# A decoder step on one core: the first weights and the first memory tile taken in smaller pieces, the second memory tile issued by SyncE, a shorter lead-in

## The chip, the core and the metric

The kernel runs on one core of one Trainium2 chip. The metric is the device time of one execution in microseconds. A core has a matrix engine (TensorE; PE in the profile, its weight loads PEld), VectorE (DVE), ScalarE (ACT), GpSimd (POOL) and SyncE (SP), which here only issues DMAs. Sixteen DMA engines move data between HBM and the on-chip memory.

## What is computed

The reference is one layer of a decoder with three parallel branches (a convolution, stick-breaking attention, softmax attention into 256 memory tokens), gates, an output projection and a feed-forward part. Cut to the part at the start of the kernel:

```python
def memory_kv(mem, g_mem, w_mem_kv, g_k_mem):
    b, m, _ = mem.shape
    kv = (rms_norm(mem, g_mem) @ w_mem_kv).reshape(b, m, 2, MEM_HEADS, HEAD_DIM)
    return rms_norm(kv[:, :, 0], g_k_mem), kv[:, :, 1]
...
        mk, mv = memory_kv(mem_prompt, g_mem[l], w_mem_kv[l], g_k_mem[l])
        yp, cp, kp, vp = trunk_layer(yp, zero_hist, no_past, no_past, mk, mv, p)
```

The memory has 256 tokens of 2048 features, and w_mem_kv is 2048 x 1024 (512 columns of keys, 512 of values). Everything is float32.

## The kernel before, in words

All weights lie in HBM as 504 slabs of 128 partitions x 1024 float32 (512 KB each), in the order of their use. A slab is loaded by SyncE (`load_slab`, line 290) into one of four raw buffers. ScalarE then casts it to a rounded high part (line 312), and VectorE subtracts the two to get the low part (line 323). The activations are split in the same way, and a product is the sum of three matmuls: high x high, low x high, high x low. Each of the three runs in the rounded format fp32r.

The first stage is `mem_products` (line 573): the memory's keys and values. The contraction runs over 16 tiles of 128 features. Two feature tiles share a pair of slabs: slab 2 k2 holds their value columns and slab 2 k2 + 1 their key columns, the first 512 columns of a slab for the even feature tile and the last 512 for the odd one. A turn is one feature tile with one slab half: six matmuls with 512 moving columns (line 594), for two blocks of 128 memory tokens. The turns begin (tile 0, values), (tile 0, keys), (tile 1, values), (tile 1, keys). So turns one and two use the first halves of slabs 0 and 1, turns three and four their second halves.

The memory tile of a feature tile is 128 x 256. `prep_mem` (line 345) scales it by the gain into a high part, for tile 0 on VectorE (line 350), for all others on ScalarE (line 354). `prep_low` (line 371) makes the low part on VectorE. The slabs of this stage are taken in two halves of 256 KB. Memory tiles 0 and 1 are loaded by two DMAs that ScalarE issues ahead of everything (lines 247 and 248); tile 0 carries 48 columns of gains. The other memory tiles are issued by SyncE (line 406), among the slab halves: memory tile, value slab half, key slab half, and so on.

TensorE begins with `warm_up` (line 1500): ten matmuls on a constant, nine of 512 columns and one of 256, whose result is not used.

The order on every engine is written out when the program is built, by a small planner (`Order`, line 76). Each job asks for an engine with an estimated cost and with flags that it waits for, and the planner runs them in simulated time. What comes out is a fixed instruction stream for each engine. The costs and flags fix the order only; on the chip, semaphores hold back an instruction until its data are there.

Of the kernel before, what the change touches and what calls it, by code (L numbers as in the profile page):

```python
# [15 lines left out]
P = 128  # L16
D_MODEL = 2048
KT = D_MODEL // P
# [8 lines left out]
ML = 256  # L27
MT = ML // P
# [8 lines left out]
SLAB = 8 * P  # L37
N_SLABS = 504


C_GMIX, C_GMEM, C_GMLP, C_BGATE = 0, 16, 32, 48
# [113 lines left out]
def dve(n, *flags, **take):  # L155
    return Ask("DVE", 0.18 + n / 920.0, flags, **take)


def act(n, *flags, **take):
    return Ask("ACT", 0.22 + n / 1200.0, flags, **take)  # L160
# [6 lines left out]
def pe(us, *flags, **take):  # L167
    return Ask("PE", us, flags, **take)


def sp(*flags, **take):
    return Ask("SP", 0.45, flags, **take)
# [7 lines left out]
MM_MEM = 0.226  # L180
# [3 lines left out]
def tile_decoder_step(ctx: ExitStack, tc: tile.TileContext, xT, memT, wall, cvec, kmat, ptab,  # L184
                      kpool, vpool, mkc, mvc, hist,
                      yT, oK, oV, oCp, oCs, oMK, oMV):
    nc = tc.nc
# [15 lines left out]
    order = Order(bufs)  # L203
    give, add, done = order.give, order.add, order.set
# [38 lines left out]
    cm = tl("k4", [P, 1024])  # L243
# [1 line left out]
    order.pools["s"].pop()  # L245
    order.pools["k4"].pop()
    nc.scalar.dma_start(cm[:, :C_BGATE + ML], memT[:, :C_BGATE + ML])
    nc.scalar.dma_start(first[:, 1], memT[:, C_BGATE + ML:C_BGATE + 2 * ML])
    nc.gpsimd.tensor_copy(cv[:, :C_BGATE], cm[:, :C_BGATE])
    km = cpool.tile([P, NKM], F32, name="km")  # L250
    pt = cpool.tile([1, 2 * NB], I32, name="pt")
# [22 lines left out]


    class Slab:
        def __init__(self, parts):
            self.parts = parts
            self.landed = [Flag() for _ in range(parts)]
            self.split = [Flag() for _ in range(parts)]  # L280

    slabs = [Slab(2 if s < 2 * KT // 2 else 1) for s in range(N_SLABS)]
    at_slab = [0, 0.0]

    def load_slab(s, part):
        sl = slabs[s]
        if part == 0:
            sl.raw = tl("wr", [P, SLAB])
        n = SLAB // sl.parts
        nc.sync.dma_start(sl.raw[:, part * n:(part + 1) * n], wall[s, :, part * n:(part + 1) * n])  # L290
        sl.landed[part].at = order.landed(n * P * 4 / 1e3)

    def shifted(p, s):
        n = 0 if s < 2 * KT // 2 else SHIFT
# [5 lines left out]
    cast_at, sub_at = [0], [0]  # L300

    def cast_weights():
        todo = [(0, 0), (1, 0), (0, 1), (1, 1)] + [(s, i) for s in range(2, N_SLABS) for i in range(slabs[s].parts)]
        for s, i in todo:
            sl = slabs[s]
            n = SLAB // sl.parts
            cast_at[0] = s
            yield act(n, sl.landed[i], **({} if i else {"w": 1}))
            if i == 0:
                sl.h = shifted("wh", s)  # L310
            c = slice(i * n, (i + 1) * n)
            nc.scalar.copy(sl.h[:, c], sl.raw[:, c])  # L312
            sl.split[i].cast = order.now.ready
            add(sub_part(s, i), lambda s=s: 0 if due(s) - order.free["DVE"] < 5.0 else 4.5)

    def sub_part(s, i):
        sl = slabs[s]
        n = SLAB // sl.parts
        yield dve(n, late=Order.HOP + 0.1)
        if i == 0:  # L320
            sl.l = shifted("wl", s)
        c = slice(i * n, (i + 1) * n)
        nc.vector.tensor_sub(sl.l[:, c], sl.raw[:, c], sl.h[:, c].bitcast(F32))  # L323
        done(sl.split[i])
        if i == sl.parts - 1:
            give("wr")

    def start_slab(s):
        at_slab[:] = [s, order.now.ready]
# [10 lines left out]
    hm, hx = [None] * KT, [None] * KT  # L340
    hm_in, hx_in = [Flag() for _ in range(KT)], [Flag() for _ in range(KT)]
    mem_sum, x_sum = [], []
    sums_m, sums_x, km_in = Flag(), Flag(), Flag()

    def prep_mem(k2, raw, here):
        for i in range(2):
            if k2 + i == 0:
                yield dve(ML, here[i], a=2)
                a = hm[0] = Acts(ML)
                nc.vector.tensor_scalar_mul(a.h, raw[:, i], cm[:, C_GMEM:C_GMEM + 1])  # L350
            else:
                yield act(ML, here[i], a=2)
                a = hm[2 * k2 + i] = Acts(ML)
                nc.scalar.mul(a.h, raw[:, i], col(C_GMEM + 2 * k2 + i))
            add(prep_low(a, raw[:, i], C_GMEM + 2 * k2 + i, ML, hm_in[2 * k2 + i]), 0.5 + 0.01 * k2)
        yield act(2 * ML, hm_in[2 * k2 + 1])
        if k2 == 0:
            mem_sum.append(tl("s", [P, 512]))
            nc.scalar.activation(mem_sum[0], raw.rearrange("p k t -> p (k t)"), AF.Square)
            give("k4")  # L360
        else:
            nc.scalar.activation(raw, raw, AF.Square)
            yield dve(2 * ML)
            nc.vector.tensor_add(mem_sum[0], mem_sum[0], raw.rearrange("p k t -> p (k t)"))
            give("s")
            if k2 == KT // 2 - 1:
                done(sums_m)
# [24 lines left out]
    def loads():  # L392

        xs = [(0, 3), (3, 6), (6, 9), (9, 12), (12, 15), (15, 16)]
        for k2 in range(KT // 2):
            raw = first
            if k2:
                yield sp(s=1)
                raw = tl("s", [P, 512]).rearrange("p (k t) -> p k t", k=2)
            here = [Flag(), Flag()]  # L400
            for i in range(2):
                for what in ("vmk" if k2 + i == 0 else "mvk"):
                    if what == "m":
                        if k2:
                            yield sp()
                            nc.sync.dma_start(raw[:, i], memT[:, C_BGATE + (2 * k2 + i) * ML:C_BGATE + (2 * k2 + i + 1) * ML])
                        here[i].at = order.landed(131)
                        if i == 0:
                            add(prep_mem(k2, raw, here), 0.5 + 0.01 * k2)
                    else:  # L410
                        yield sp(**({} if i else {"wr": 1}))
                        load_slab(2 * k2 + "vk".index(what), i)
            if k2 >= 1 and xs:
                k0, k1 = xs.pop(0)
                yield sp(k4=1)
                x = tl("k4", [P, 1024])[:, :(k1 - k0) * T].rearrange("p (k t) -> p k t", k=k1 - k0)
                nc.sync.dma_start(x, xT[:, k0:k1, :])
                there = Flag()
                there.at = order.landed(147 * (k1 - k0))
                for k in range(k0, k1):  # L420
                    add(prep_x(k, x[:, k - k0], there, k == k1 - 1), 1.5 + 0.01 * k)
            if k2 == 1:
                yield sp()
                nc.sync.dma_start(cv[:, C_BGATE:], cvec[:, C_BGATE:])
            if k2 == 2:
                yield sp()
                nc.sync.dma_start(km, kmat)
                km_in.at = order.landed(213)
                yield sp()
                nc.sync.dma_start(pt, ptab)  # L430
                pt_in.at = order.landed(1) + 20.0
        for s in range(KT, N_SLABS):
            yield sp(wr=1)
            load_slab(s, 0)
# [138 lines left out]
    def mem_products():  # L573
        yield pe(0.0, pm=4)
        pv, pk = [bank("pm") for _ in range(MT)], [bank("pm") for _ in range(MT)]
        add(mem_values(pv), 1.0)
        add(mem_keys(pk), 0.9)
        turns = [(0, 0), (0, 1), (1, 0), (1, 1)]
        turns += [(2 * k2 + i, x) for k2 in range(1, KT // 2) for x in range(2) for i in range(2)]
        slab_no[0] += KT  # L580
        for k, x in turns:
            ps, flag = ((pv, vflag), (pk, kflag))[x]
            s = 2 * (k // 2) + x
            sl = slabs[s]
            w = slice(k % 2 * MW, (k % 2 + 1) * MW)
            yield pe(6 * MM_MEM, sl.split[k % 2], hm_in[k])
            if k % 2 == 0:
                start_slab(s)
            a = hm[k]
            todo = [(a.h, sl.h, 0), (a.h, sl.h, 1), (a.l, sl.h, 0), (a.l, sl.h, 1), (a.h, sl.l, 0), (a.h, sl.l, 1)]  # L590
            if k == 0:
                todo = todo[:2] + todo[4:] + todo[2:4]
            for j, (y, z, m) in enumerate(todo):
                nc.tensor.matmul(ps[m], y[:, m * P:(m + 1) * P], z[:, w],  # L594
                                 start=(k == 0 and j < 2), stop=(k == KT - 1 and j in (4, 5)))
            if k % 2:
                give("w")
            if k == KT - 1:
                done(flag)
            if k % 2 and x:  # L600
                give("a", 4)
# [897 lines left out]

    def warm_up():  # L1500

        yield pe(4.2, pa=1)
        junk = bank("pa")
        one = nc.const_aps.tensor(1.0, [P, 512], mybir.dt.bfloat16)
        for n in [512] * 9 + [256]:
            nc.tensor.matmul(junk[:, :n], one[:, :P], one[:, :n], start=True, stop=True)
        give("pa")

# [201 lines left out]
```

## Time and profile before

| What | Value |
|---|---|
| Median of 3 runs | 1618.26 us (1618.14 to 1618.41) |
| Span of the profiled execution, first to last instruction | 1616.7 us |
| TensorE busy in the span | 1612.4 us, 12657 matmuls |
| VectorE busy | 1003.4 us |
| ScalarE busy | 771.5 us |
| GpSimd busy | 138.4 us |
| Moved by DMA | 310.25 MB, mean 192 GB/s |

The times in the profile count from the first instruction of the execution. In a row of a timeline stand the start, the duration, the engine, the line of the kernel, the operation, the tile written and the tiles read, and in brackets how long the engine was idle before it and what ended that. A q behind the name of an engine means that its sequencer issues a DMA. The shares of busy time are means over the whole span; for a change of the first microseconds it is the rows of the first microseconds that matter, and what follows on the chain of work that ended last.

### The profile page before, as it was taken

Reading aid. Unit: us, or ns where it says so; the run is one execution under the profiler, and the core shown is the slowest. Engines: PE = TensorE matmul, PEld = TensorE weight load, DVE = VectorE, ACT = ScalarE, POOL = GpSimd, SP = SyncE. Lnnn points to the kernel's source line nnn. Section 1 sums busy time; section 2 is a strip of 40 time slices with the busy share of each in tenths; the row PEclk is TensorE's granted clock in tenths of the full one; section 3 lists DMA queues with packets and bytes.
Section 4 is the critical chain, followed back from the end, with each engine's and each line's share of the span. In section 5 each row is a group of like instructions: output and inputs, shape, how many; then the busy total and the mean of one; then the engine's idle time right before and its main releaser. Section 6 shows DMA issues by size and latency. Waiting matters only on the chain.

```text
span 1616.7 us, 30794 instructions
## 1 busy us (share of the span) xinstructions
PE 1612.4 (100%) x12657; PEld 1595.2 (99%) x12657; DVE 1003.4 (62%) x1469; ACT 771.5 (48%) x1106; POOL 138.4 (9%) x107
## 2 busy tenths in 40 slices
PE   9999999999999999999999999999999999999999
PEld 7999999999999999999999999999999999999999
DVE  7999888887777655655555544555445554455443
ACT  8856887775433634444443333333333333333332
POOL 0020000000000000002222100121002210022100
PEclk9999999999999999999999999999999999999999
DMA  9898678978755555566655555555555555555563
GB/s 325 224 211 279 174 224 245 342 213 296 217 171 162 166 176 171 152 192 193 192 172 169 170 170 170 170 170 170 169 169 168 171 168 167 172 165 168 180 192 100
DMA packets 127200, 310.25 MB, mean 192 GB/s; under 512 B 40018, under 2 KB 49618, under 8 KB 127058
## 3 DMA queue, kind: packets, MB, share of 16 engines
q1 hardware_dynamic: 126770, 307.98, 63.0%
q8 instruction: 99, 1.62, 0.4%
q14 instruction: 43, 0.35, 0.1%
q10 hardware_dynamic: 288, 0.29, 0.1%
HBM read 296.99 MB, written 6.32 MB: 188 GB/s over the span
## 4 chain that ended last, share of the span: by engine, by line
PE 99%; DMA 0%; ACT 0%; DVE 0%; issue 0%
PE pm L541 93%; PE pm L594 3%; PE pa L541 1%; PE pl L1102 1%; PE pl L1286 0%; PE pa L929 0%; DMA wr<-in_wall 0%; PE pa L930 0%; PE pa L931 0%; PE pl L1116 0%; PE pa L1226 0%; PE pa L1262 0%; PE pa L889 0%; ACT wh L312 0%; DVE a L1456 0%; PE pl L1324 0%
## 5 line engine op out<-in xcount | busy, mean ns | idle before, releaser
L312 ACT CAST wh<-wr 128x1024 fp32r<-128x1024 f32 (+1 forms) x520 | 530.6, 1023 | 628.3 <-PE pm L541 568.8
L541 PE MATMUL pm<-a,wh 128*128 128x288 f32 x5184 | 735.2, 292 | 0.0
L323 DVE TENSOR_TENSOR wl<-wr,wh 128x1024 fp32r<-128x1024 f32 (+1 forms) x520 | 618.3, 1192 | 185.5 <-ACT wh L312 181.6
L541 PEld LDWEIGHTS pm<-a,wh 128*128 128x128 f32 x5184 | 695.4, 188 | 0.4 <-issue 0.4
L541 PE MATMUL pm<-a,wl 128*128 128x288 f32 x2592 | 395.3, 292 | 0.0
L541 PEld LDWEIGHTS pm<-a,wl 128*128 128x128 f32 x2592 | 357.5, 188 | 0.2 <-issue 0.2
L541 PE MATMUL pm<-k,wh 128*128 128x288 f32 x2400 | 337.8, 292 | 0.0
L541 PEld LDWEIGHTS pm<-k,wh 128*128 128x128 f32 x2400 | 321.0, 188 | 0.0
L541 PE MATMUL pm<-k,wl 128*128 128x288 f32 x1200 | 182.0, 292 | 0.0
L541 PEld LDWEIGHTS pm<-k,wl 128*128 128x128 f32 x1200 | 165.1, 188 | 0.0
L1442 POOL TENSOR_TENSOR t<-t 128x288 f32<-128x288 f32 x64 | 95.6, 1495 | 600.4 <-DVE t L1439 600.4
L1456 DVE TENSOR_TENSOR a<-a,pm 128x288 f32<-128x288 f32 x64 | 29.1, 455 | 122.7 <-PE pm L541 122.7
L1439 DVE SCALAR_TENSOR_TENSOR t<-pm,rx 128x288 f32<-128x288 f32 x64 | 29.2, 458 | 90.7 <-PE pm L541 90.7
L1445 ACT CAST k<-t 128x288 fp32r<-128x288 f32 x60 | 25.8, 432 | 123.4 <-POOL t L1442 123.4
L1358 DVE TENSOR_TENSOR t<-pm,rx 128x288 f32<-128x288 f32 x48 | 22.0, 458 | 68.3 <-PE pm L541 68.3
L1447 DVE TENSOR_TENSOR k<-t,k 128x288 fp32r<-128x288 f32 x60 | 27.8, 466 | 58.2 <-ACT k L1445 58.2
L773 DVE SCALAR_TENSOR_TENSOR a<-a,cv,a 128x256 f32<-128x256 f32 x120 | 59.6, 496 | 1.3
L1428 POOL TENSOR_TENSOR t<-t,t 128x288 f32<-128x288 f32 x15 | 21.6, 1440 | 416.1 <-ACT t L1425 416.1
L594 PE MATMUL pm<-wh,a 128*128 128x512 f32 x128 | 34.6, 393 | 0.3 <-ACT wh L312 0.3
L541 PE MATMUL pm<-s,wh 128*128 128x288 f32 x160 | 33.7, 292 | 0.0
L594 PEld LDWEIGHTS pm<-wh,a 128*128 128x128 f32 x128 | 24.2, 190 | 5.9 <-ACT wh L312 1.0
L541 PEld LDWEIGHTS pm<-s,wh 128*128 128x128 f32 x160 | 25.3, 188 | 0.0
(203 smaller groups left out, 756.7 us busy)
## 6 DMA issues: line engine op xcount, KB each, us to landing
wr<-in_wall SPq DMA_DIRECT2D x488, 512.0 KB, 3.7
wr<-in_wall SPq DMA_DIRECT2D x32, 256.0 KB, 5.1
k<-in_kpool SPq DMA_DIRECT2D x32, 256.0 KB, 5.9
k<-in_vpool SPq DMA_DIRECT2D x32, 256.0 KB, 5.9
k<-in_mkc SPq DMA_DIRECT2D x8, 512.0 KB, 7.4
k<-in_mvc SPq DMA_DIRECT2D x8, 512.0 KB, 7.7
t<-in_xT SPq DMA_DIRECT2D x16, 144.0 KB, 3.7
out_yT<-a SPq DMA_DIRECT2D x16, 144.0 KB, 1.9
```

Of the source, the lines that this page charges most:

```text
L312: nc.scalar.copy(sl.h[:, c], sl.raw[:, c])
L323: nc.vector.tensor_sub(sl.l[:, c], sl.raw[:, c], sl.h[:, c].bitcast(F32))
L541: nc.tensor.matmul(ps, w, a, start=(first and i == 0), stop=(last and i == len(todo) - 1))
L594: nc.tensor.matmul(ps[m], y[:, m * P:(m + 1) * P], z[:, w], start=(k == 0 and j < 2), stop=(k == KT - 1 and j in (4, 5)))
L773: nc.vector.scalar_tensor_tensor(c[:, :NP], up[:, k:k + NP], w, c[:, :NP], op0=ALU.mult, op1=ALU.add)
L1358: nc.vector.tensor_mul(g, ps, rx)
L1428: nc.gpsimd.tensor_add(sq_sum[0], sq_sum[0], res[0])
L1439: nc.vector.scalar_tensor_tensor(r, ps, 0.0, r2, op0=ALU.max, op1=ALU.mult)
L1442: nc.gpsimd.tensor_mul(r, r, r)
L1445: nc.scalar.copy(a.h, r)
L1447: nc.vector.tensor_sub(a.l, r, a.h.bitcast(F32))
L1456: nc.vector.tensor_add(x1[j], x1[j], ps)
```

## The change

1. The DMA for memory tile 1 goes from ScalarE to SyncE. It is now SyncE's fifth DMA, behind four pieces of slabs 0 and 1.
2. Slabs 0 and 1 are taken in pieces of 256, 256 and 512 columns in place of two halves of 512. Each piece has its own load, cast and subtraction. Other slabs are cut as before.
3. The scaling of memory tile 0 is cut into two pieces of 128 tokens.
4. The high x high matmuls of the first two turns are cut into halves of 256 columns. Each half waits for the cast of its own piece. After them come the two matmuls with the low weights and then the two with the low memory tile. The order of the three kinds is as before in turns one and two.
5. The warm-up has eight matmuls (seven of 512 columns and one of 256) and 3.2 us in the planner's estimate in place of 4.2.

The core of the diff:

```diff
     nc.scalar.dma_start(cm[:, :C_BGATE + ML], memT[:, :C_BGATE + ML])
-    nc.scalar.dma_start(first[:, 1], memT[:, C_BGATE + ML:C_BGATE + 2 * ML])
...
+    def ends_of(s):
+        return [256, 512, SLAB] if s < 2 else [512, SLAB] if s < KT else [SLAB]
+
+    slabs = [Slab(ends_of(s)) for s in range(N_SLABS)]
...
-        todo = [(0, 0), (1, 0), (0, 1), (1, 1)] + [(s, i) for s in range(2, N_SLABS) for i in range(slabs[s].parts)]
+        todo = [(0, 0), (0, 1), (1, 0), (1, 1), (0, 2), (1, 2)]
+        todo += [(s, i) for s in range(2, N_SLABS) for i in range(slabs[s].parts)]
...
             if k2 + i == 0:
-                yield dve(ML, here[i], a=2)
+                yield dve(P, here[i], a=2)
                 a = hm[0] = Acts(ML)
-                nc.vector.tensor_scalar_mul(a.h, raw[:, i], cm[:, C_GMEM:C_GMEM + 1])
+                for m in range(MT):
+                    if m:
+                        yield dve(P)
+                    t = slice(m * P, (m + 1) * P)
+                    nc.vector.tensor_scalar_mul(a.h[:, t], raw[:, i, t], cm[:, C_GMEM:C_GMEM + 1])
+                done(scaled)
...
-                        if k2:
+                        if k2 + i:
                             yield sp()
                             nc.sync.dma_start(raw[:, i], memT[:, C_BGATE + (2 * k2 + i) * ML:C_BGATE + (2 * k2 + i + 1) * ML])
...
-            yield pe(6 * MM_MEM, sl.split[k % 2], hm_in[k])
+            if k == 0:
+                for i in range(2):
+                    yield pe(MM_MEM, sl.cast[i], scaled)
+                    if i == 0:
+                        start_slab(s)
+                    for m in range(MT):
+                        c = sl.cols[i]
+                        nc.tensor.matmul(ps[m][:, c], hm[0].h[:, m * P:(m + 1) * P], sl.h[:, c],
+                                         start=(i == 0), stop=False)
+                a = hm[0]
+                for y, z, flags in ((a.h, sl.l, sl.split[:2]), (a.l, sl.h, hm_in[:1])):
+                    yield pe(2 * MM_MEM, *flags)
+                    for m in range(MT):
+                        nc.tensor.matmul(ps[m], y[:, m * P:(m + 1) * P], z[:, w], start=False, stop=False)
+                continue
+            yield pe(6 * MM_MEM, sl.split[k % 2 + (s < 2)], hm_in[k])
...
-        yield pe(4.2, pa=1)
+        yield pe(3.2, pa=1)
         junk = bank("pa")
         one = nc.const_aps.tensor(1.0, [P, 512], mybir.dt.bfloat16)
-        for n in [512] * 9 + [256]:
+        for n in [512] * 7 + [256]:
```

More of the change, by code (lines that the diff above doesn't have):

```diff
@@ L276, in tile_decoder_step, with __init__ @@
     class Slab:
[L277 to L282, printed above, removed]
+        def __init__(self, ends):
+            self.parts = len(ends)
+            self.cols = [slice(a, b) for a, b in zip([0] + ends, ends)]
+            self.landed, self.cast, self.split = ([Flag() for _ in ends] for _ in range(3))
+    def ends_of(s):
+        return [256, 512, SLAB] if s < 2 else [512, SLAB] if s < KT else [SLAB]
+    slabs = [Slab(ends_of(s)) for s in range(N_SLABS)]
     at_slab = [0, 0.0]
@@ L288, in load_slab @@
             sl.raw = tl("wr", [P, SLAB])
-        n = SLAB // sl.parts
-        nc.sync.dma_start(sl.raw[:, part * n:(part + 1) * n], wall[s, :, part * n:(part + 1) * n])
-        sl.landed[part].at = order.landed(n * P * 4 / 1e3)
+        c = sl.cols[part]
+        nc.sync.dma_start(sl.raw[:, c], wall[s, :, c])
+        sl.landed[part].at = order.landed((c.stop - c.start) * P * 4 / 1e3)
     def shifted(p, s):
@@ L302, in cast_weights @@
     def cast_weights():
-        todo = [(0, 0), (1, 0), (0, 1), (1, 1)] + [(s, i) for s in range(2, N_SLABS) for i in range(slabs[s].parts)]
+        todo = [(0, 0), (0, 1), (1, 0), (1, 1), (0, 2), (1, 2)]
+        todo += [(s, i) for s in range(2, N_SLABS) for i in range(slabs[s].parts)]
         for s, i in todo:
             sl = slabs[s]
-            n = SLAB // sl.parts
+            c = sl.cols[i]
             cast_at[0] = s
-            yield act(n, sl.landed[i], **({} if i else {"w": 1}))
+            yield act(c.stop - c.start, sl.landed[i], **({} if i else {"w": 1}))
             if i == 0:
                 sl.h = shifted("wh", s)
-            c = slice(i * n, (i + 1) * n)
             nc.scalar.copy(sl.h[:, c], sl.raw[:, c])
-            sl.split[i].cast = order.now.ready
+            done(sl.cast[i])
             add(sub_part(s, i), lambda s=s: 0 if due(s) - order.free["DVE"] < 5.0 else 4.5)
@@ L317, in sub_part @@
         sl = slabs[s]
-        n = SLAB // sl.parts
-        yield dve(n, late=Order.HOP + 0.1)
+        c = sl.cols[i]
+        yield dve(c.stop - c.start, late=Order.HOP + 0.1)
         if i == 0:
             sl.l = shifted("wl", s)
-        c = slice(i * n, (i + 1) * n)
         nc.vector.tensor_sub(sl.l[:, c], sl.raw[:, c], sl.h[:, c].bitcast(F32))
@@ L343, in tile_decoder_step @@
     sums_m, sums_x, km_in = Flag(), Flag(), Flag()
+    scaled = Flag()
     def prep_mem(k2, raw, here):
@@ L411, in loads @@
                         yield sp(**({} if i else {"wr": 1}))
-                        load_slab(2 * k2 + "vk".index(what), i)
+                        s = 2 * k2 + "vk".index(what)
+                        mine = [part for part, c in enumerate(slabs[s].cols) if c.start // 512 == i]
+                        for part in mine:
+                            if part != mine[0]:
+                                yield sp()
+                            load_slab(s, part)
             if k2 >= 1 and xs:
@@ L585, in mem_products @@
             w = slice(k % 2 * MW, (k % 2 + 1) * MW)
-            yield pe(6 * MM_MEM, sl.split[k % 2], hm_in[k])
+            if k == 0:
[4 more added lines that the diff above has]
+                    for m in range(MT):
+                        c = sl.cols[i]
+                        nc.tensor.matmul(ps[m][:, c], hm[0].h[:, m * P:(m + 1) * P], sl.h[:, c],
[7 more added lines that the diff above has]
+            yield pe(6 * MM_MEM, sl.split[k % 2 + (s < 2)], hm_in[k])
             if k % 2 == 0:
@@ L590, in mem_products @@
             todo = [(a.h, sl.h, 0), (a.h, sl.h, 1), (a.l, sl.h, 0), (a.l, sl.h, 1), (a.h, sl.l, 0), (a.h, sl.l, 1)]
-            if k == 0:
-                todo = todo[:2] + todo[4:] + todo[2:4]
             for j, (y, z, m) in enumerate(todo):
                 nc.tensor.matmul(ps[m], y[:, m * P:(m + 1) * P], z[:, w],
-                                 start=(k == 0 and j < 2), stop=(k == KT - 1 and j in (4, 5)))
+                                 start=False, stop=(k == KT - 1 and j in (4, 5)))
             if k % 2:
```

## The prediction

> **What bounds the kernel now.** I read the page first, then the waits of TensorE, then the chain that ended last in order of time.
>
> ```profile
> span 1616.7 us, 30794 instructions
> ```
>
> ```profile
> PE pa L1506 <- PEq L1687: 0.8, 1, 0.8
> PE pm L594 <- ACT wh L312: 0.3, 1, 0.3
> ```
>
> ```profile
> 0.75 3.81 DMA wr<-in_wall
> ...
> 5.31 44.23 PE pm L594 x192
> ...
> 1613.57 0.45 DVE a L1456
> ```
>
> The second fence is the whole answer for TensorE: it waited before its warm-up and once, 0.3 us, before its first product. The chain says the same: one DMA, one cast, then products from 5.31 us to 1613.57 us, and a tail of 3.1 us (1616.7 - 1613.57). So 1608.3 us of the 1616.7 are TensorE at work, and the change leaves every one of those products in place (the first two turns are only cut differently). What it can move is when that run starts and how much it stumbles at first. The span is 1616.7 us and the median of the runs 1618.26 us, so 1.6 us lie around the span; I make the sum in the span and carry its difference to the median.
>
> For the start I read the timeline of the first 9 us, the spread of the line of the first products, and SyncE's waits up to 8 us.
>
> ```profile
> 0.75 1.81 SPq L290 DMA_DIRECT2D wr<-in_wall  x4
> 0.77 0.40 ACTq L247 DMA_DIRECT2D k<-in_memT  x1
> 0.78 4.21 PE L1506 MATMUL pa<-const-bfloat16-1.0 128*128 128x512 bf16 x10 [0.78 <-PEq L1687]
> 1.20 0.45 ACTq L248 DMA_DIRECT2D k<-in_memT  x1
> 2.61 0.43 SPq L406 DMA_DIRECT2D s<-in_memT  x1
> 3.08 1.82 SPq L290 DMA_DIRECT2D wr<-in_wall  x2
> 4.58 0.62 ACT L312 CAST wh<-wr 128x512 fp32r<-128x512 f32 x1 [2.56 <-DMA wr<-in_wall]
> 4.76 0.40 DVE L350 TENSOR_SCALAR a<-k 128x256 fp32r<-128x256 f32 x1 [2.97 <-DMA k<-in_memT]
> ...
> 5.23 0.69 DVE L323 TENSOR_TENSOR wl<-wr,wh 128x512 fp32r<-128x512 f32 x1
> ...
> 5.31 1.01 PE L594 MATMUL pm<-wh,a 128*128 128x512 f32 x2 [0.32 <-ACT wh L312]
> 5.84 0.48 DVE L371 SCALAR_TENSOR_TENSOR a<-k,cv,a 128x256 fp32r<-128x256 f32 x1
> ...
> 6.13 0.62 ACT L312 CAST wh<-wr 128x512 fp32r<-128x512 f32 x1 [0.93 <-DMA wr<-in_wall]
> 6.16 0.62 PE L594 MATMUL pm<-wl,a 128*128 128x512 f32 x2
> ...
> 6.62 1.07 PE L594 MATMUL pm<-wh,a 128*128 128x512 f32 x4
> ...
> 8.09 1.55 PE L594 MATMUL pm<-wh,a 128*128 128x512 f32 x6
> ```
>
> ```profile
> L594 PE MATMUL pm<-wh,a x128: 388/389/767, 5.3 to 48.7; 128*128 128x512 f32 x128
> ```
>
> ```profile
> SPq L290 <- DMA wr<-in_wall: 0.9, 1, 0.9
> ```
>
> Three things stand in these rows. First, a steady product costs 44.23/192 = 0.23 us. The first turn starts at 5.31, the second at 6.62 + 2 x 0.23 = 7.08, the third (slab 0's second half) at 8.09 + 2 x 0.23 = 8.55. Twelve products are worth 2.76 us and took 3.24, so 0.48 us are lost in the first two turns. Second, most of that loss is a slow TensorE: the two products at 5.31 took 0.85 until the next one at 6.16 instead of 0.46, and the longest product lasted 767 ns against a median of 389. The warm-up ran at that slow pace too: 4.21 us for 9.5 pieces of 512 columns are 0.44 each. So here full pace came about 6.0, some 5.2 us after the first warm-up matmul. Third, eight DMAs (SyncE's first six and ScalarE's two) went out unhindered; the ninth, the second of the row at 3.08, waited 0.9 us for a landing.
>
> **The change part by part.** Durations of the cut pieces come from the groups of the first 75 us, with shapes kept apart, and the pace of the transfers from the window of 2 to 3 us (its last column, GB/s).
>
> ```profile
> L323 DVE TENSOR_TENSOR wl<-wr,wh 128x512 fp32r<-128x512 f32 x32 | 21.1, 688 | 3.4 <-ACT wh L312 3.0
> L312 ACT CAST wh<-wr 128x512 fp32r<-128x512 f32 x32 | 18.7, 612 | 5.8 <-DMA wr<-in_wall 5.5
> L323 DVE TENSOR_TENSOR wl<-wr,wh 128x1024 fp32r<-128x1024 f32 x11 | 13.4, 1223 | 0.7 <-ACT wh L312 0.7
> L312 ACT CAST wh<-wr 128x1024 fp32r<-128x1024 f32 x11 | 11.5, 1042 | 2.9 <-PE pm L541 2.9
> ```
>
> ```profile
> 2.00:3.00 1.00, 1.00 (x4) 0.42 (x3) 0.00 (x0) 0.02 (x1) 0.00 (x0) 1.00 0.76 205
> ```
>
> ```profile
> wr<-in_wall SPq DMA_DIRECT2D x32, 256.0 KB, 5.1
> ...
> s<-in_memT SPq DMA_DIRECT2D x14, 128.0 KB, 4.9
> ```
>
> From 512 to 1024 columns the cast grows by 0.430 us and the subtraction by 0.535, so a piece of 256 columns costs 0.612 - 0.215 = 0.40 on ScalarE and 0.688 - 0.268 = 0.42 on VectorE. Each extra cut thus adds 0.18 of fixed cost to a cast and 0.15 to a subtraction. The scaling of 256 columns in 0.40 becomes two of 128, 0.27 each by the same slope.
>
> *Landing of the first piece and of memory tile 0.* The first slab half landed at 4.56 (0.75 + 3.81), the tile just before 4.76. Now 128 KB less stand beside the tile, and its neighbour on ScalarE's queue is gone. From above: if the 128 KB fewer shorten the landing by their whole time at the slow pace of the third microsecond, 205 GB/s, it comes 128/205 = 0.62 us earlier. From below: no earlier, since a 128 KB load lands 4.9 us after issue in the median and a 256 KB load 5.1. I take 0.3, nearer to the lower end, because those two rows barely differ. Landings, then: piece about 4.25, tile about 4.45.
>
> *First turn.* VectorE scales at 4.46 to 4.73 and 4.73 to 5.00, subtracts at 5.00 to 5.42 and 5.42 to 5.84, and makes the low part at 5.84 to 6.32 (0.48). ScalarE casts at 4.27 to 4.67 and, the second piece having landed, to 5.07. Before, the first product stood 0.11 after the cast; so the first one now starts at 4.84, 0.47 earlier. Its four half products, at 0.22 each while TensorE is slow, are done by 5.7; the two products with the low weights wait for 5.84, run from 5.93 to 6.39, and the two with the low tile, ready at 6.32, to 6.85. The second turn starts at 6.85 instead of 7.08. VectorE has become what the turn waits for: its extra instructions (0.14 for the scaling, 0.15 for the subtraction) eat the 0.3 us of the landing, and the low part ends at 6.32 just as before.
>
> *Second turn.* ScalarE's cast waited until 6.13 for slab 1's first half; in two pieces, and with 128 KB of the tile now behind it, I take 5.9 for the second piece, cast by 6.3, well before 7.1. VectorE subtracts 6.32 to 6.74 to 7.16; the low weights are wanted at 6.85 + 0.46 = 7.31. So this turn runs freely and the third starts at 6.85 + 6 x 0.23 = 8.23 instead of 8.55: 0.32 us gained. Its bounds are about 0 (no earlier landing, next part) and 0.64 (0.32 + 0.32, a landing 0.62 early).
>
> *Second memory tile.* ScalarE loses an issue of 0.45 at 1.20, when it was idle until 4.58: nothing. SyncE gets it as its fifth DMA, at 0.75 + 4 x 0.45 = 2.55 instead of ScalarE's 1.20. By the 4.9 us row it lands at 7.45 at worst; scaling (0.5) and low part (0.48) end by 8.45, wanted at 8.23 (high) and 8.69 (low). The high part ends at 7.95. Covered; without that cover it would cost the third turn a microsecond at most.
>
> *SyncE's queue.* Three more issues stand ahead of memory tile 2: 0.75 + 7 x 0.45 = 3.9 instead of 2.61. It is also now the ninth DMA, so it waits for the first landing, about 4.25, and the loads of slabs 2 and 3 queue behind it. The worst landing of the tile is 4.3 + 4.9 = 9.2, of slab 2's half, one landing later, 4.6 + 5.1 = 9.7. They are used at 8.23 + 12 x 0.23 = 11.0. Cast (0.61) and subtraction (0.69) end by 11.0, and the subtracted part is needed four products later. Covered, by the same bytes still queued.
>
> *Later.* Slabs 2 on keep their halves and order. If TensorE is 0.3 us early, transfers that set their own time must still be in front. The tightest row that I found in the first stage is slab 8's second half:
>
> ```profile
> 27.75 0.62 ACT L312 CAST wh<-wr 128x512 fp32r<-128x512 f32 x1 [1.12 <-DMA wr<-in_wall]
> ```
>
> ```profile
> 28.97 0.39 PE L594 MATMUL pm<-wh,a 128*128 128x512 f32 x1
> ```
>
> The cast ends at 28.37, the product starts at 28.97: 0.6 us, of which 0.3 would go and 0.1 is handover. It holds.
>
> *Lead-in.* Two matmuls at 0.44 go: the warm-up ends at 4.99 - 0.89 = 4.10 instead of 4.99. It is not on the path itself. The gap before the first product becomes 4.84 - 4.10 = 0.74 instead of 0.32. I take the pace to come near 6.0 as before, at no cost.
>
> Sum: 1618.26 - 0.32 = 1617.9 us (span 1616.4). What a measurement of this kernel can tell from no change is about 0.2%, 3.2 us, so this counts as the same. Even a start right at the first landing could not gain 3.2.
>
> **The rivals.**
>
> *Nothing lands earlier* (the cut does not do what it says). For it: 4.9 against 5.1 us for half the bytes, and seven issues at 0.45 behind each other. Against it: less is queued beside the tile. Then VectorE starts at 4.76, the third turn at 8.53, and the time is 1618.2.
>
> *TensorE stays slow* (ends slower than before). The row of 767 ns shows that the pace at 5.31 was still the slow one after 4.21 us of warm-up and a gap of 0.32. With 3.3 us and a gap of 0.74 it may need the same 5.2 us anew from the first product: until 4.84 + 5.2 = 10.0. At half pace 2.6 us of work are done by then, where the forecast has 2.76 + (10.0 - 8.23) = 4.5: 1.9 us worse, 1619.8. It decides if the interrupted warm-up does not count; half the price, 1618.9, if full pace comes halfway through. The Trainium skill ("TensorE: Matmul & The Clock Gate", section on the clock gate) says the clock doubles only after a free-running window of about 3.4 us of sustained matmuls, and that the moment varies from run to run. By that rule a lead-in of 3.3 us fills no window on its own, and slow products until 4.84 + 3.4 = 8.2 would leave 1.7 us of work done instead of 2.76, and give 1619.0. The trace agrees on the two paces (0.44 and 0.23); the granted clock of that window reads 1.00 all the same, so the moment shows only in the durations.
>
> *The order written later is worse.* The planner's clock shifts by some tenths, so casts and subtractions among the attention work may swap. A half slab issued only when TensorE has run dry costs 5.1 us to land, 0.61 to cast and 0.69 to subtract, 6.4 in all: 1624. It decides once a load falls behind by its whole lead of four buffers. Against it: TensorE's waits list nothing after the first product.
>
> **How the numbers follow.** Forecast 0.58, nothing earlier 0.17, slow TensorE 0.20 (the gap doubles and the lead-in shrinks, but one slow start was already there and passed), worse order 0.05. The range takes the forecast's gains to 0.64, widened by the 0.27 us between the fastest and the slowest of the runs before (1618.14 to 1618.41), and most of the slow case: 1617.3 to 1619.6. Faster by over 0.2% needs 3.2 us out of a start of 5.31 that must hold a landing: 0.01. Slower by over 0.2% is the worse order: 0.05. The rest, 0.94, is within 0.2%.
>
> **What would show it.** Right: first product near 4.84, third turn near 8.2, the half products slow and the full ones from 6 us at 0.23, VectorE without idle time from 4.5 to 7.2, no TensorE wait after 9 us. Wrong: the first scaling still at 4.76; products at 0.44 beyond 7 us; memory tile 2 or slab 2 as what a product waits for; a TensorE wait on a cast or a subtraction anywhere later.

## The result and the profile after

| | before | after |
|---|---|---|
| median of 5 runs | 1618.26 us (1618.14 to 1618.63) | 1627.24 us (1625.73 to 1628.02) |
| span of the profiled execution | 1616.7 us | 1624.5 us |

The ratio is 1.0053, with a 95% interval of 1.0042 to 1.0063. The change made the kernel 9 us slower, and the runs spread over 2.3 us instead of 0.5. In the profile, 7.8 us of it can be looked for. Of all the executions reported below one, the last of e11's eleven, took 3259.07 us, twice the others; the record has no trace of it, and the ranges leave it out. TensorE's waits, the whole answer for the kernel after (engine, tile and line, what it waited for, us in total, times, longest):

```profile
PE pm L606 <- DVE a L357: 2.0, 2, 1.2
PE pm L554 <- ACT a L1058: 1.4, 1, 1.4
PE pa L1532 <- PEq L1713: 0.8, 1, 0.8
PE pm L554 <- DVE a L1060: 0.3, 1, 0.3
```

Two waits are new. One is at the start, for the scaling of memory tile 0 (line 357 of the new kernel). The other is on lines 1058 and 1060, which split the attention output of the samples (`out_rows`). That has nothing to do with the lines of the change. The first place, in the timeline of the first 12 us:

```profile
0.78 3.36 PE L1532 MATMUL pa<-const-bfloat16-1.0 128*128 128x512 bf16 x8 [0.78 <-PEq L1713]
...
3.65 0.92 ACT L314 CAST wh<-wr 128x256 fp32r<-128x256 f32 x2 [1.62 <-DMA wr<-in_wall]
3.87 0.22 POOL L248 COPY cv<-k 128x48 f32<-128x48 f32 x1 [2.47 <-DMA k<-in_memT]
...
4.08 0.94 DVE L324 TENSOR_TENSOR wl<-wr,wh 128x256 fp32r<-128x256 f32 x2 [2.30 <-ACT wh L314]
...
4.94 0.28 DVE L357 TENSOR_SCALAR a<-k 128x128 fp32r<-128x128 f32 x1
...
5.37 0.55 PE L606 MATMUL pm<-wh,a 128*128 128x256 f32 x1 [1.23 <-DVE a L357]
...
5.47 0.95 DVE L324 TENSOR_TENSOR wl<-wr,wh 128x256 fp32r<-128x256 f32 x2 [0.25 <-ACT wh L314]
...
6.34 0.28 DVE L357 TENSOR_SCALAR a<-k 128x128 fp32r<-128x128 f32 x1
...
6.67 1.01 PE L606 MATMUL pm<-wh,a 128*128 128x256 f32 x3 [0.75 <-DVE a L357]
...
10.89 1.05 PE L612 MATMUL pm<-wh,a 128*128 128x512 f32 x2
...
11.75 0.47 PE L620 MATMUL pm<-wh,a 128*128 128x512 f32 x1
```

The memory tile has landed by 3.87, when GpSimd's copy from it starts; before, it landed just ahead of 4.76. That is an early landing indeed. But VectorE subtracts both pieces of slab 0 first and scales only at 4.94. Then it subtracts both pieces of slab 1, whose data it has to wait for, and scales the second half at 6.34. So the first product starts at 5.37, as late as before, and the second at 6.67. From there no wait is listed, yet the two products at 10.89 take until 11.75, 0.43 each instead of 0.23: TensorE runs at its slow pace up to the third turn. That turn starts at 11.75, and before it was 8.55. The start costs 3.2 us.

The second place. From the chain that ended last (start, duration, what), the third group of the sample attention, one row of the kernel before:

```profile
422.83 3.70 PE pl L1102 x128
```

and of the kernel after, with what follows it:

```profile
458.00 3.70 PE pl L1128 x128
461.70 6.45 PE pm L554 x48
468.21 0.34 issue
468.55 0.47 DVE a L799
469.02 1.14 DVE wl L324
470.16 0.40 DVE a L799
470.59 0.48 DVE a L799
471.23 59.07 PE pm L554 x435
```

The same group stands 35 us later in the kernel after. Its output is taken by products whose place among the weights is fixed. They came up 48 matmuls later and had to wait: between 468.2 and 471.2 the chain runs over VectorE. The windows of this place (us, then busy time and count of TensorE; the third number from the end is the granted clock):

```profile
460.00:468.00 8.00, 8.00 (x111) 7.80 (x103) 4.72 (x9) 2.59 (x4) 0.00 (x0) 1.00 0.41 114
468.00:472.60 4.60, 2.94 (x17) 2.02 (x15) 4.39 (x13) 2.84 (x10) 0.00 (x0) 1.00 0.51 158
472.70:476.10 3.40, 3.40 (x15) 3.40 (x15) 2.13 (x5) 1.05 (x1) 0.00 (x0) 0.50 0.12 49
476.20:480.00 3.80, 3.80 (x31) 3.80 (x31) 2.66 (x6) 1.05 (x1) 0.00 (x0) 1.00 0.41 110
```

After the wait the granted clock falls to 0.50 for 3.4 us: 15 matmuls in 3.4 us instead of some 28 (31 in 3.8). At 0.13 us each, that is 1.7 us; the wait itself costs 17 matmuls in 4.6 us instead of 37, 2.6 us. By this estimate the place costs about 4.3 us, and 3.2 + 4.3 = 7.5 of the 7.8.

### The profile page after: what moved, and what is told of

Read it like the earlier page. It is cut to its first block, busy times and chain, and to the rows that moved or that the text cites. A ratio compares the mean times of both kernels' runs of the same rounds, so it can differ in the third digit from the quotient of the medians.

```text
span 1624.5 us, 30801 instructions
## 1 busy us (share of the span) xinstructions
PE 1616.7 (100%) x12659; PEld 1598.8 (98%) x12659; DVE 1004.3 (62%) x1472; ACT 773.7 (48%) x1110; POOL 137.9 (8%) x107
## 3 DMA queue, kind: packets, MB, share of 16 engines
q8 instruction: 99, 1.62, 0.4%
## 4 chain that ended last, share of the span: by engine, by line
PE 99%; DVE 0%; DMA 0%; SPq 0%; issue 0%; ACT 0%
PE pm L554 93%; PE pm L620 3%; PE pa L554 1%; PE pl L1128 1%; PE pl L1312 0%; PE pa L955 0%; PE pa L957 0%; PE pa L956 0%; PE pl L1142 0%; PE pm L612 0%; DMA wr<-in_wall 0%; PE pm L606 0%; PE pa L1252 0%; PE pa L1288 0%; DVE wl L324 0%; DVE a L799 0%
## 5 line engine op out<-in xcount | busy, mean ns | idle before, releaser
L314 ACT CAST wh<-wr 128x1024 fp32r<-128x1024 f32 (+2 forms) x522 | 530.7, 1019 | 627.1 <-PE pm L554 555.0
L324 DVE TENSOR_TENSOR wl<-wr,wh 128x1024 fp32r<-128x1024 f32 (+2 forms) x522 | 621.0, 1193 | 193.4 <-ACT wh L314 191.1
```

## The experiments

The theory after this reading: two separate losses. The start is lost to VectorE's order and to a slow TensorE. The late loss comes from the order that the planner wrote, not from the late start. In what follows "big matmuls" are those of the two product lines (541 and 594 of the kernel before), counted in the written order of TensorE. The third sample group stands after 2778 of them in the kernel before and after 3028 in the kernel after. The times of before beside these runs have medians of 1618.33 to 1618.41 us.

**e1, the lead-in of before in the kernel after.**

```diff
-        yield pe(3.2, pa=1)
+        yield pe(4.2, pa=1)
-        for n in [512] * 7 + [256]:
+        for n in [512] * 9 + [256]:
```

> The change with the lead-in of before (ten matmuls, 4.2 us for the planner); the written order after the lead-in stays that of the change. Theory (two losses: the start, made of VectorE's order and of a slow TensorE after the short lead-in, some 3.3 us; and a stall near 468 us that the written order brings, with a slow stretch behind it, some 4.5 us): full pace comes some 3 to 4 us earlier, the third turn starts near 9.3 us instead of 11.75, the late stall stays: 1622.5 to 1625. Rival (the start is lost to VectorE's order alone, the lead-in costs nothing): third turn stays beyond 11 us, 1626 to 1628.

Measured: 1627.25 us (ratio 1.0055, interval 1.0041 to 1.0068), so the rival's number, with the third turn at 11.21. The profile shows why, in its windows and in one row of its timeline:

```profile
7.24 0.62 PE L606 MATMUL pm<-wh,a 128*128 128x256 f32 x3 [1.66 <-DVE a L357]
```

```profile
5.20:8.50 3.30, 1.62 (x8) 1.31 (x9) 2.24 (x6) 1.94 (x5) 0.00 (x0) 1.00 1.00 341
8.60:12.00 3.40, 3.40 (x11) 2.83 (x10) 2.69 (x6) 2.96 (x7) 0.00 (x0) 0.50 0.98 362
12.10:14.00 1.90, 1.90 (x10) 1.59 (x9) 1.90 (x4) 1.60 (x4) 0.00 (x0) 1.00 1.07 377
```

TensorE had reached its full pace (the two products at 7.69 took 0.23 each), but it had waited 1.66 us for the second scaling, was busy for only 1.62 of 3.30 us, and ran at half clock for the next 3.4. The longer lead-in is undone by VectorE's order. My theory was wrong in giving the lead-in a price of its own here, the rival in thinking that the pace plays no part.

**e2, the scaling in one step of the planner.** Two instructions as before, but nothing can come between them.

```diff
-                yield dve(P, here[i], a=2)
+                yield dve(ML, here[i], a=2)
...
-                    if m:
-                        yield dve(P)
```

> The change with the scaling of memory tile 0 asked for in one step of the planner (two instructions right behind each other). The planner then writes the later order of before again (third sample group after 2782 of the big matmuls instead of 3028). Theory: the late stall goes (4.5 us), of the start only a part, since the lead-in stays short: 1620 to 1622. Rival (the late stall comes from a start that is 3 us late against its transfers, whatever the order): a stall of over 1 us stays, 1624 or more.

Measured: 1620.46 us (1619.26 to 1621.66; ratio 1.0013, interval 1.0004 to 1.0022). That is inside the theory's range, and in its profile no wait is left after the start. One intermediate step of the planner, 0.3 us of work, accounts for 6.8 us of the 9, through the start and through the order written later together.

**e3, the later order in the kernel before.** The kernel before, with one word of the loading order changed, so that the planner reckons memory tile 0 ahead of slab 0. Transfers, pieces and lead-in stay. The third sample group stands after 3024 of the big matmuls.

```diff
-                for what in ("vmk" if k2 + i == 0 else "mvk"):
+                for what in "mvk":
```

> The kernel before, with one edit of the planner: memory tile 0 is reckoned to land ahead of slab 0. Transfers, pieces and lead-in of before; the written order from the end of the first stage on becomes that of the change (third sample group after 3024 of the big matmuls instead of 2778). Theory: start as before, a stall of some 3 us near 465 us and slow products behind it: 1621.5 to 1624. Rival (the order is harmless): 1618.0 to 1618.6.

Measured: 1622.62 us (ratio 1.0026, interval 1.0015 to 1.0036), 4.2 over before. Its waits hold the late one, of the same size, and one of 0.9 us near 55 us that is its own:

```profile
PE pm L541 <- ACT a L1032: 1.4, 1, 1.4
PE pm L541 <- ACT a L644: 0.9, 1, 0.9
...
PE pm L594 <- DVE wl L323: 0.4, 1, 0.4
```

The last row shows that the start is not quite that of before. The edit also puts tile 0's low part ahead of the first subtraction on VectorE, so TensorE waits 0.4 us for its first low weights, and the third turn starts at 8.78 instead of 8.55. The 0.9 us near 55 us and these 0.2 us are part of the 4.2. Here too the granted clock falls to 0.50 behind the late wait. A start that is 3 us late is not needed for it; the written order is enough.

**e4, the short lead-in alone.** The kernel before with eight warm-up matmuls; the planner's estimate, and so the order, unchanged.

> The kernel before with eight warm-up matmuls in place of ten; the written order is that of before throughout. Theory: the gap before the first product grows from 0.3 to 1.2 us, full pace comes one window of activity later (about 3.4 us) in most executions: first product unmoved at 5.3, 1619 to 1620, with a wider spread between runs than before. Rival (the lead-in costs nothing): 1618.0 to 1618.6, spread as before.

Measured: median 1618.38 us (1618.15 to 1619.91; ratio 1.0004, interval 0.9995 to 1.0013). The eleven runs fall into two groups: six between 1618.15 and 1618.38, five between 1619.36 and 1619.91. So the short lead-in costs about 1.4 us in about half of the executions and nothing in the others, and a median hides it. The profile is of the faster group; where the slower one loses its time was not seen.

**e5 and e6, the scaling first.** The kernel after with the edit of e3, which puts both scalings and the low part ahead of the subtractions; e6 has the lead-in of e1 as well. In both the third sample group stands after 2782.

> The change with one edit of the planner: memory tile 0 is reckoned to land ahead of slab 0, so both scalings and the low part stand ahead of the subtractions on VectorE; short lead-in, later order as before (third sample group after 2782). Theory (the start is lost to VectorE's order; the short lead-in costs its 1.4 us only in some of the executions): first product near 4.4, third turn near 8.1 at full pace: 1617.7 to 1618.0 in the good executions, 1619.2 to 1619.6 in the others. Rival (smaller pieces give nothing, the data of the second turn bind): 1618.2 to 1618.6 in the good ones.

> As the kernel with memory tile 0 reckoned first, with the lead-in of before (ten matmuls, 4.2 us). Theory: the lead-in ends at 4.99, first product right behind it, third turn near 8.1, no gap for the pace to fall back in: 1617.7 to 1618.0 with a spread as before. Rival: 1618.2 to 1618.6, since the product data of the second turn come no earlier.

Measured: e5 1618.87 us (1618.43 to 1620.21; interval 0.9996 to 1.0014), e6 1618.84 (1618.28 to 1619.81; interval 0.9994 to 1.0012). The loss of 9 us is gone and no gain shows. Both expectations were missed: the better executions of e5 (eight of eleven) lie between 1618.43 and 1619.01, over the theory's range and all but one over the rival's, and e6 has its median over both ranges and a spread of 1.5 us, twice that of before. In e5's profile the first product does start at 4.09, but the first turn then waits for its low weights, and the second half of the second turn for slab 1's second piece:

```profile
4.09 1.06 PE L606 MATMUL pm<-wh,a 128*128 128x256 f32 x4
...
6.31 0.41 ACT L314 CAST wh<-wr 128x256 fp32r<-128x256 f32 x1 [0.78 <-DMA wr<-in_wall]
...
6.51 0.76 PE L606 MATMUL pm<-wh,a 128*128 128x256 f32 x4
```

```profile
PE pm L612 <- DVE wl L324: 0.3, 1, 0.3
```

The first product is 1.2 us early and the second turn starts at 6.51, 0.6 before the old 7.08. Half of the gain is gone by then, in part to that wait: VectorE makes the low weights only after both scalings and the low part. The second piece of slab 1 lands no earlier than its first half did before (6.13), and the third turn starts at 8.27, 0.3 before the old 8.55. In e6 the second and third turns start at 6.63 and 8.54. A wait of 0.4 us near 55 us, at the same place as in e3, takes back more there.

**e7, the second memory tile by SyncE, alone.** The kernel before with the first part of the change only.

> The kernel before with one part of the change: memory tile 1 issued by SyncE, behind the first halves of slabs 0 and 1. Written order on TensorE as before. Theory (the early landing of memory tile 0 in the change, 3.8 instead of 4.7 us, comes from ScalarE's second DMA being gone): memory tile 0 lands near 4.2, its first product starts some 0.3 earlier, total 1618.0 to 1618.4. Rival (it comes from the smaller pieces): tile 0 lands at 4.6 to 4.8, total 1618.2 to 1618.8.

Measured: 1617.73 us (1617.62 to 1618.34; ratio 0.9997, interval 0.9988 to 1.0006), 0.6 less than the 1618.33 of before beside it (1618.0 to 1618.76). The interval holds 1, so a gain is likely and not shown; the median lies below both expected ranges. Its start:

```profile
4.05 0.62 ACT L311 CAST wh<-wr 128x512 fp32r<-128x512 f32 x1 [2.02 <-DMA wr<-in_wall]
4.23 0.40 DVE L349 TENSOR_SCALAR a<-k 128x256 fp32r<-128x256 f32 x1 [2.45 <-DMA k<-in_memT]
...
4.78 0.85 PE L593 MATMUL pm<-wh,a 128*128 128x512 f32 x2
```

In this execution both tile 0 and slab 0's half are there 0.5 us sooner than before, and the first product starts at 4.78. e11 and e12 show below that this is not yet the cause of the change's early landing.

**e8, the scaling in one step, and the lead-in of before.**

> The change with the scaling in one step of the planner and the lead-in of before (ten matmuls, 4.2 us). The subtractions of slab 0 still stand ahead of the scalings, the subtractions of slab 1 ahead of the low part. Theory: first product near 5.2, third turn near 9.2 as in the one-step kernel at full pace, 1619.2 to 1619.6 and few executions above. Rival (the spread of the one-step kernel, 1619.3 to 1621.7, is not of the lead-in): median 1620.5, same spread.

Measured: 1619.51 us (1619.17 to 1619.75; interval 0.9998 to 1.0016), inside the theory's range. Against e2 the longer lead-in saves 0.95 us and takes the spread from 2.4 us to 0.6. Where the products no longer wait on a second scaling, the lead-in has the price that it lacked in e1.

**e9 and e10, the sample attention moved in the kernel after.** Only its rank in the planner is changed; the start is untouched.

```diff
-        add(samples(), 2.3)
+        add(samples(), 2.0)
```

(2.6 in e10.)

> The change with one edit of the planner: the sample attention is added at rank 2.0 instead of 2.3, so its third group stands after 2980 of the big matmuls instead of 3028, some 6 us earlier; the start is untouched. Theory (the stall near 468 us is this group arriving too late for the branch products that use it): the stall and the slow stretch behind it go, 1622.3 to 1623.3. Rival (the late loss hangs on something else in that written order): 1626 or more.

> The change with the sample attention at rank 2.6: its third group stands after 3082 of the big matmuls instead of 3028, 7 us later, which is about where its output is used. Theory: TensorE waits longer at that place, 8 to 10 us instead of 2.7, 1632 to 1636. Rival (the late loss hangs on something else): 1626 to 1628.5.

Measured: e9 1622.46 us (1622.26 to 1623.64; ratio 1.0027, interval 1.0017 to 1.0037), e10 1670.95 us (1669.36 to 1673.0). The waits of e9:

```profile
PE pm L606 <- DVE a L357: 3.5, 2, 2.3
PE pa L1532 <- PEq L1713: 0.8, 1, 0.8
PE pm L554 <- DVE a L1060: 0.3, 1, 0.3
```

With the group 48 matmuls earlier, the wait for line 1058 is gone, and with it 4.8 us. What is left over before, 4.1 us, is mostly the start: in e9's profile the products wait even longer for the second scaling, and the third turn starts at 12.02, 3.5 us later than before. The 0.3 us for line 1060 are what remains of the late place.

```profile
7.94 1.01 PE L606 MATMUL pm<-wh,a 128*128 128x256 f32 x3 [2.28 <-DVE a L357]
```

e10 went the way that was expected and far beyond it, 43.7 us over the kernel after where 9 at most were expected: it was no clean dose, since the whole of the sample attention moved and TensorE then waited at several places. Its longest:

```profile
PE pl L1128 <- DVE k L1588: 11.3, 1, 11.3
PE pm L554 <- ACT a L1058: 8.4, 3, 3.2
PE pm L554 <- DVE a L1240: 7.0, 1, 7.0
```

**e11, tile 1 by SyncE and the scaling in two instructions**, in one step of the planner; the slabs in halves.

> The kernel before with memory tile 1 issued by SyncE and the scaling of tile 0 in two instructions right behind each other; slabs in halves of 512 columns, lead-in of before, later order of before. Theory (the pieces of 256 columns, not the split scaling, hold the scale-first kernels at 1618.8): 1617.5 to 1617.9, as with tile 1 by SyncE alone. Rival (the split scaling costs VectorE what tile 1 by SyncE gains): 1618.4 or more.

Measured: median 1618.06 us (ten of the eleven executions between 1617.61 and 1618.26; ratio 0.9997, interval 0.9988 to 1.0006), between the two ranges, 0.3 over e7 and 0.8 under e6. Against the kernel before beside it, the ratio is that of e7. The cut scaling shows no gain. In its profile tile 0 is scaled from 4.73 on, 0.5 later than in e7 with the same transfers, so single executions differ by that much in their first landings.

**e12, the pieces and half products with tile 1 still on ScalarE**, scaling in one step and first, lead-in of before.

> The pieces of 256 columns and the half products with tile 1 still issued by ScalarE, lead-in of before, memory tile 0 reckoned first, scaling in one step, later order of before. Theory (small pieces bring slab 1's first half later): its second piece lands at 6.3 us or later, third turn at 8.6 or later, 1618.5 to 1619.3. Rival (small pieces land early and pay): 1617.5 to 1618.0.

Measured: 1618.56 us (1618.13 to 1618.87; interval 0.9992 to 1.001), inside the theory's range, but not for its reason. In the profile the second piece of slab 1 is cast from 5.78 on, and the third turn starts at 8.03:

```profile
3.73 0.53 DVE L356 TENSOR_SCALAR a<-k 128x128 fp32r<-128x128 f32 x2 [1.94 <-DMA k<-in_memT]
...
5.78 0.41 ACT L315 CAST wh<-wr 128x256 fp32r<-128x256 f32 x1 [0.20 <-DMA wr<-in_wall]
...
8.03 1.08 PE L619 MATMUL pm<-wh,a 128*128 128x512 f32 x4
```

So small pieces do not bring slab 1 late here. The first row settles something else: tile 0 is there at 3.73 although tile 1 still stands behind it on ScalarE's queue. In all nine profiles with small pieces GpSimd's copy from the tile starts between 3.6 and 3.9, in the five with halves between 4.3 and 4.8, wherever tile 1 is issued. The early landing goes with the pieces, and e7's theory of it does not hold.

What holds the kernels with small pieces (e5, e6, e12) 0.8 to 1.1 us above e7 is answered in part. Their first turn takes 2.0 to 2.4 us in the profiles, against 1.7 in e7 (from 4.78 to 6.48), with a wait of 0.3 us for the low weights in each. The rest stays open.

## Why the prediction was wrong

**The step that failed first** is the first turn: "VectorE scales at 4.46 to 4.73 and 4.73 to 5.00, subtracts at 5.00". I took the order of the kernel before and cut its instructions into pieces. But the order on VectorE is written by the planner, which knows no landings, only its own estimates. With the pieces it wrote the first subtractions ahead of the scaling (with tile 0 reckoned to land first, in e5, it wrote them the other way round); and since the second scaling had become a request of its own, two more subtractions came between. On the chip the scaling could have started at 3.87; it started at 4.94 and 6.34. With that order undone, nearly all of the start comes back: the third turn starts at 8.27 in e5 and 8.54 in e6, against 11.75 in the kernel after, 12.02 in e9 and 8.55 before.

**The landing** was mis-sized: I took 0.3 us, bounded by 0.62, and the tile landed about 0.9 earlier. From the medians of 128 and 256 KB loads I had leaned to the low end; those are medians over the first stage, and the first 256 KB load took 3.8 us and not 5.1. The landing goes with the small pieces: 3.6 to 3.9 with them, e12 included, where ScalarE still issues its second transfer. What that transfer is worth alone is open, since with halves and without it the tile was there at 4.23 in e7 and at 4.73 in e11.

**The second turn** "runs freely" held as far as waits go, but at the slow pace: it took 2.56 us (9.19 to 11.75) where 1.38 were forecast. The first turn took 3.82 where 2.01 were forecast, from a start that was 0.53 late.

**The lead-in** was put down "at no cost". It costs 1.4 us in five of eleven executions by itself (e4) and 0.95 in the median of e2 against e8, and nothing where a later wait loses the clock anyway (e1). The rival on a slow TensorE had the slow products right, but put them down to the short lead-in; with the long one the waits on the scaling cost the pace as well (e1). Its worst time of 10.0 for full pace was passed: at 10.89 the products still took 0.43, and full pace came near 12. The Trainium skill ("TensorE: Matmul & The Clock Gate", section on the clock gate) gives a window of about 3.4 us. The traces agree on that length: the clock of 0.50 lasted 3.4 us in e1 and again behind the late wait. But the Trainium skill has the clock fall, in the same section, after an idle window, and here windows in which TensorE was still busy for half to two thirds of the time (1.62 of 3.30 us in e1, 2.94 of 4.60 at 468) were followed by it; the measurement decides.

**"Later"** looked at the transfers of the first stage and found 0.6 us of room. It looked at the wrong thing: what moved was the order of ScalarE, VectorE and SyncE far behind. I had that as the last rival, with a chance of 0.05, and priced it as a late slab. The late part was not a slab but the sample attention, at 4.3 us with the slow stretch behind it. The chance was set by how quiet TensorE was in the kernel before, where this group stood some 290 matmuls ahead of its use. That room was no property of the kernel; it belonged to one written order, and one word in the load loop takes it away (e3).

**What held:** the warm-up ended at 4.14 (4.10 forecast), memory tile 2 was issued at 4.04 by SyncE (forecast 3.9, or 4.25 by the wait), and neither of the transfers that were moved on SyncE became what a product waits for. Of the 9 us, about 4.8 are the late wait with its slow stretch (after against e9), and about 4.1 are left, most of them the start (e9 against before; 3.2 to 3.5 us at the third turn in the profiles). Of these 4.1, 2 us go with the extra step of the scaling (e9 against e2), 1 with the short lead-in (e2 against e8), and 0.7 with the subtractions ahead of the scaling (e8 against e6); 0.5 is left and not settled. These are differences of medians, and the first one also holds what remains of the late place in e9.

## What to carry to other kernels

Where a planner writes the order, a change of the first microseconds is a change of the whole program: build the order and compare it far from the edit, and look at how much room the late consumers have, before costing anything. An instruction that is cut in two for an earlier start needs its halves held together, or the planner may put other work between them. In the kernel after and in e1, a wait of some 1.7 us on the matrix engine cost itself and, behind it, about as much again at half clock.

## What the runs showed of the hardware

The granted clock falls to 0.50 for 3.4 us after a wait of only 1.66 us (e1) or 1.4 plus 0.3 us (after, e3). I had thought of the slow pace as a matter of the start alone. In e2 a wait of 0.8 us was not followed by it; the two products at 8.26 take 0.23 each:

```profile
7.23 0.72 PE L610 MATMUL pm<-wh,a 128*128 128x512 f32 x2 [0.84 <-DVE a L377]
...
8.26 0.63 PE L610 MATMUL pm<-wl,a 128*128 128x512 f32 x2
8.73 0.62 PE L610 MATMUL pm<-wh,a 128*128 128x512 f32 x2
```

Where the limit lies between the two was not measured.

Full pace at the start does not come at a fixed moment. The same ten warm-up matmuls took 4.21 us in before, e7, e8 and e11, 4.05 in e6 and 3.71 in e3 and e12. Five of eleven runs of e4 are 1.4 us longer than the other six; that this is the same thing is likely and not shown.

The first memory tile was there between 3.6 and 3.9 us in every profile in which SyncE's first loads were of 128 KB, and between 4.3 and 4.8 in every one in which they were of 256 KB (by the start of GpSimd's copy from it).
